# Branch A's product moved from the merge stage to the attention stage, and the order of the other two branches exchanged

## The chip, the cores and the metric

The kernel runs on one core of one Trainium2 chip. The metric is the device time of one execution in microseconds. Before the change it was 2761.7 us, the median of three runs (2759.91 to 2764.09).

The engines are called by their names in the profile: PE (TensorE, matmuls), PEld (the loading of its weights), DVE (VectorE), ACT (ScalarE), POOL (GpSimd) and SP (the engine that issues every DMA of this kernel, in one queue). Each engine works its own queue in order; semaphores tie the queues together.

## The reference

A block of two layers runs over 768 tokens: 256 of a context and 512 latent ones. Each layer projects its normalised input once, feeds three mixers, gates and sums their outputs, and goes on to an output projection and an MLP. What matters here:

```python
for l in range(DEPTH):                       # DEPTH = 2
    ...
    ya, yc = attend_queries(proj, ...)       # A: grouped-query attention, C: latent attention, 512 channels each
    ...
    ys = s5_glu(ys, u, s5_d[l], s5_w_glu[l]) # B: state-space scan, then gelu, product, a * sigmoid(g)
    mix = merge_branches(proj, ya, ys, yc, lp)
    x_mid = post_norm(x, g1 * mix, ...)
    ff = squared_relu_mlp(...)

def merge_branches(proj, ya, ys, yc, lp):
    g = sigmoid(proj[..., OFF_GATE:]).reshape(bsz, L, 3, 1024)
    merged = (g[..., 0, :] * (ya @ w_branch_a)
              + g[..., 1, :] * (ys @ w_branch_s5)
              + g[..., 2, :] * (yc @ w_branch_c))
    return merged @ w_out
```

Layer 0 computes all 768 tokens; layer 1 needs the output of the 512 latent ones only.

## The kernel before

**Products.** Channels lie on the partitions, tokens along the free dimension. Every large product is done in three passes of fp32r: weights and inputs are each split into a high part (a cast on ACT, line 151 for weights) and a low part (a subtraction, line 124 on DVE or line 154 on POOL), and `mm3` (lines 165 to 169) issues high x high, high x low and low x high into one PSUM group. `weights` (line 131) loads a block of weights into a `wr` tile and splits it into `wh` and `wl` tiles.

**Stages of a layer.** `layer` (line 362) runs the projections, then the attention stage (lines 1385 to 1404), then the merge stage (1407 to 1430), then `tail` with the output projection and the MLP. The layer's input lies in two tiles of [128, 8, 768], a high and a low half, in the pool `hp` with tag `h` and two buffers (lines 177 and 1247). The gates are the last to read them.

**Attention stage.** `attention` (line 913) runs through 8 heads of branch A, then 8 heads of branch C, block by block of 256 queries: scores on PE (line 872), maximum on DVE (875), exponential on ACT (878), scaling on DVE (880), transposes on PE (891), split on ACT and DVE (893, 894), product with V on PE (903, 904), sum of the halves (908, 909) and, for each second head, a DMA of the `yst` tile to the branch's DRAM tensor `brd[0]` or `brd[2]` (911). Beside it, `filler` (line 1398) issues the gates that the projection stage left over (`gates`, line 1122: blocks 9 to 23 in layer 0, 10 to 23 in layer 1; a block is 24 matmuls for each chunk of tokens, a tanh on ACT at line 1132 and a DMA to the DRAM tensor `gd`) and the S5 readout (`s5_readout`, line 1046: eight steps of copies on POOL, 24 small matmuls at lines 1070 and 1073, and an evacuation on ACT at line 1075 that goes to `Yd`). All gate blocks but one stand ahead of the readout in the program, the last behind it. Gates, S5 states and readout share the PSUM pool `gate`, which has one bank here (line 1394). Before the readout can start, a scan of 95 steps on POOL must have ended (lines 1036 to 1043).

**Merge stage.** `merge_branches` (line 1136) takes the branches in the order 0 (A), 1 (B), 2 (C). For A and C it loads the 512 channels from `brd` as four tiles `gt` and splits them (1152, 1153). For B it calls `s5_glu` (line 1079), which loads the readout from `Yd`, computes gelu with ACT and DVE (1088 to 1094), multiplies by the GLU's weights and forms the gated output (1096 to 1115). Then each branch runs 8 blocks of 128 output channels: 12 matmuls per chunk of tokens (chunks are two of 384 in layer 0 and one of 512 in layer 1, line 1119), a load of the gate tile `sg`, and an evacuation on DVE (line 1171) that multiplies by one plus the gate's tanh. Branch A's result begins the eight tiles `part`; B and C add theirs on POOL (1175); C, as the last, also splits the sum into `merged` (1177). In layer 0, the scalars of the next layer's S5 (`s5_scalars`, a long chain of small DVE operations) are issued after 12 steps of the merge, and a modulation (`mods`, line 278, lines 309 and 329) runs beside the rest.

**What sets the order.** The program's order gives each instruction a priority; `later` (line 107) lowers it. A planner works through a simulated timeline and puts, on each engine, the ready instruction of best priority next; the resulting queues are fixed. `mixed` (line 46) sets the program's order: it interleaves generators by the cost that they yield, divided by a weight. Buffers of a pool are taken in turn, and a tile that lies in memory of a closed pool waits for the tiles that lay there.

Of the kernel before, what the change touches and what calls it, by code (L numbers as in the profile page):

```python
# [13 lines left out]
F32 = mybir.dt.float32  # L14
F32R = mybir.dt.float32r
AF = mybir.ActivationFunctionType
ALU = mybir.AluOpType
# [4 lines left out]
P = 128  # L22
D = 1024
SEQ = 512
CTX = 256
T = SEQ + CTX
NT = T // P
EPS = 1e-6
DEPTH = 2
ALPHA = float((2.0 * DEPTH) ** 0.25)  # L30
GRID_W = 64
NCH = T // 8
# [13 lines left out]
def mixed(*gens):  # L46

    live = [[g, w, 0.0] for g, w in gens]
    while live:
        live.sort(key=lambda e: e[2])  # L50
        e = live[0]
        try:
            v = next(e[0])
        except StopIteration:
            live.remove(e)
            continue
        e[2] += v / e[1]
        yield v
# [7 lines left out]
def merge(*gens):  # L66
    drain(mixed(*gens))


class Block:  # L70
# [1005 lines left out]
            self.dma(out=self.Yd[:, 4 * q:4 * q + 4, 0:nn], in_=y)  # L1076
            yield 4.0

    def s5_glu(self, act, pool, l, out):

        nc = self.nc
        n0 = 0 if l < DEPTH - 1 else CTX // 8
        nn = NCH - n0
        glu = []
        for q in range(4):
            yt, t1, t2 = (self.tok(self.sgp, tag="gt").rearrange("p (i n) -> p i n", i=8) for _ in range(3))
            self.dma(out=yt, in_=self.Yd.rearrange("(i c) g n -> (c g) i n", c=16)[q * P:(q + 1) * P, :, 0:nn])
            nc.scalar.activation(t1, yt, AF.Square)
            nc.vector.tensor_scalar(out=t1, in0=t1, scalar1=0.044715, scalar2=1.0, op0=ALU.mult, op1=ALU.add)
            nc.vector.tensor_tensor(out=t1, in0=t1, in1=yt, op=ALU.mult)  # L1090
            nc.scalar.activation(t2, t1, AF.Tanh, scale=float(np.sqrt(2.0 / np.pi)))
            nc.vector.scalar_tensor_tensor(out=t1, in0=t2, scalar=1.0, in1=yt, op0=ALU.add, op1=ALU.mult)
            gH, gL = (self.tok(pool, F32R).rearrange("p (i n) -> p i n", i=8) for _ in range(2))
            self.half_split(gH, gL, t1)
            glu.append((gH, gL))
        wsrc = self.I["w_glu"][l].rearrange("(k p) (h c) -> p k h c", p=P, h=2)
        step = 4 if nn == NCH else 8
        for m in range(4):
            w = self.weights(([(h, wsrc[:, :, h, m * P:(m + 1) * P]) for h in range(2)], [P, 4, 2, P]), 256)
            ys = self.tok(self.sgp, tag="ys")  # L1100
            yv = ys.rearrange("p (n i) -> p i n", i=8)[:, ::-1, :]
            for i0 in range(0, 8, step):
                pss = []
                for h in range(2):
                    ps = self.bank([P, step, nn])
                    self.mm_k(ps, [([x[:, h, :] for x in w[k]], [x[:, i0:i0 + step, :] for x in glu[k]])
                                   for k in range(4)])
                    pss.append(ps)
                t1 = self.tok(self.sgp, tag="gt")[:, 0:step * nn].rearrange("p (i n) -> p i n", n=nn)
                nc.scalar.activation(t1, pss[1], AF.Tanh, scale=0.5)  # L1110
                nc.vector.scalar_tensor_tensor(out=yv[:, i0:i0 + step, :], in0=t1, scalar=1.0, in1=pss[0],
                                               op0=ALU.add, op1=ALU.mult)
            yh, yl = self.tok(act, F32R), self.tok(act, F32R)
            self.half_split(yh, yl, ys)
            out.append((yh, yl))
            yield 3.0
# [5 lines left out]
    def gates(self, l, hT, blocks, pools):  # L1122

        nc = self.nc
        for m in blocks:
            g0 = OFF_GATE + m * P
            wg = self.weights(self.I["w_in"][l, :, g0:g0 + P].rearrange("(k p) c -> p k c", p=P), P, pools)
            for t0, n in self.chunks(l):
# [4 lines left out]
                self.dma(out=self.gd[m, :, t0:t0 + n], in_=sg)  # L1133
                yield 24 * n / 2500.0

    def merge_branches(self, l, act, pool, merged):

        nc = self.nc
        c0 = self.chunks(l)[0][0]
        part = [None] * 8  # L1140
        for n, b in enumerate((0, 1, 2)):
            if b == 1:
                y = []
                yield from self.s5_glu(act, pool, l, y)
            else:
                y = []
                for k in range(4):
                    raw = self.tok(self.sgp, tag="gt")
                    self.dma(out=raw, in_=self.brd[b][k * P:(k + 1) * P, c0:])
                    yp = act if n == 0 else pool  # L1150
                    yh, yl = self.tok(yp, F32R), self.tok(yp, F32R)
                    nc.scalar.copy(yh, raw)  # L1152
                    self.split_low(yl, raw, yh)
                    y.append((yh, yl))
            wb = self.I[("wba", "wbs", "wbc")[b]][l].rearrange("(k p) c -> p k c", p=P)
            for m in range(8):
                if m % 2 == 0:
                    wbu = self.weights(wb[:, :, m * P:(m + 2) * P], 256)
                sg = self.tok(self.sgp, tag="sg")
                self.dma(out=sg, in_=self.gd[b * 8 + m, :, c0:])  # L1160
                if n == 0:
                    part[m] = self.tok(pool)
                if n == 2:
                    merged.append((self.tok(act, F32R), self.tok(act, F32R)))
                for t0, cnt in self.chunks(l):
                    ts = slice(t0 - c0, t0 - c0 + cnt)
                    pr = self.bank([P, cnt])
                    ms = slice((m % 2) * P, (m % 2) * P + P)
                    self.mm_k(pr, [([w[:, ms] for w in wbu[k]], [x[:, ts] for x in y[k]]) for k in range(4)])
                    o = part[m][:, ts] if n == 0 else sg[:, ts]  # L1170
                    nc.vector.scalar_tensor_tensor(out=o, in0=sg[:, ts], scalar=1.0, in1=pr, op0=ALU.add,
                                                   op1=ALU.mult)
                    if n == 0:
                        continue
                    nc.gpsimd.tensor_tensor(out=part[m][:, ts], in0=part[m][:, ts], in1=sg[:, ts], op=ALU.add)
                    if n == 2:
                        self.half_split(merged[m][0][:, ts], merged[m][1][:, ts], part[m][:, ts])
                yield 1.5


    def bcast_row(self, rows, src):
# [180 lines left out]
    def layer(self, l, hT, stop):  # L1362
        nc = self.nc
        last = l == DEPTH - 1
        nx = (9, 10)[l]
        with ExitStack() as c1:
# [18 lines left out]
            with ExitStack() as c2:  # L1385
# [10 lines left out]
                drain(self.s5_states(sp, l, slots))  # L1396

                def filler():
                    half = nx + (14, 13)[l]
                    yield from self.later(self.gates(l, hT, range(nx, half), wg), 200)  # L1400
                    yield from self.later(self.s5_readout(sp, l, slots), 0)
                    yield from self.later(self.gates(l, hT, range(half, 24), wg), 200)

                merge((self.attention(arena, l, per), 235.0 if not last else 180.0), (filler(), (170.0, 100.0)[l]))
        if stop == f"attn{l}":
            return
        self.c0 = c0 = self.chunks(l)[0][0]
        with ExitStack() as c1:
# [5 lines left out]
            with ExitStack() as c2:  # L1414
# [5 lines left out]
                if not last:  # L1420
                    for _ in range(12):
                        next(main)
                    self.s5_scalars(sp, _Carve(self, self.sgp, "gt"), l + 1)
                work = [(main, 42.0)]
                if not last:
                    self.mod_pools(c2, 2, 1)
                    self.lows = (1, 2)
# [113 lines left out]
```

## Time and profile before

| | |
|---|---|
| median of three runs | 2761.7 us |
| the profiled execution | 2761.72 us, its span 2759.9 us |
| mean granted clock of PE | 0.962 |
| first score product of the attention, layer 0 | 412.0 us |
| last write of the attention's output, layer 0 and layer 1 | issued at 790.66 and 2228.45 us |
| first product of the merge, layer 0 and layer 1 | 793.05 and 2227.65 us |
| first product with the output weights, layer 0 | 944.72 us |
| last evacuation of the merge (line 1171), layer 1 | 2327.34 us |

Times inside the execution count from the first instruction. A row of the stretches gives, for each engine, its busy time in the stretch and the number of its instructions; the granted clock is the share of full speed at which PE was let run. A row of the timeline gives start, duration, engine, line, operation, output and inputs, and in brackets how long the engine had been idle before it and what ended that. A row of the groups gives all instructions of one line and shape: busy time and mean duration in ns, then the idle time before them and what ended it. Matmuls are pipelined: their durations overlap, and the distance from start to start is what one costs.

### The profile page before, as it was taken

The page shows a single profiled execution, that of the slowest core. Times are in us where ns is not written, and L with a number is a line of the kernel's source. Part 1 is how long each engine was busy: PE and PEld are TensorE (multiplying, and loading weights), DVE is VectorE, ACT ScalarE, POOL GpSimd, SP SyncE. Part 2 cuts the span into 40 slices and gives each one's busy share as a digit, 9 for nine tenths or more (in the row PEclk, how much of TensorE's full clock was granted, in tenths as well). Part 3 has the DMA queues.
Part 4 walks back from the last instruction along what each step waited for, and adds up shares of the span by engine and source line. Part 5 has one row for each costly group of instructions (what it writes and reads, how often), then busy time and mean ns, then how long its engine had stood idle before and what let it go on. Part 6 is the DMA issues. An engine that isn't in the chain of part 4 may idle for free.

```text
span 2759.9 us, 45140 instructions
## 1 busy us (share of the span) xinstructions
PE 2570.2 (93%) x16128; PEld 2380.6 (86%) x16128; DVE 1794.7 (65%) x3338; ACT 1197.2 (43%) x2420; POOL 1167.4 (42%) x1698
## 2 busy tenths in 40 slices
PE   7999998999899989999999988998998989799997
PEld 4989898999899878999999988997877868688886
DVE  7998535777778678456668574455766757844345
ACT  4333367655543235132322234457654633533332
POOL 2378313870202577445446361310785004722224
PEclk9989998999999999999999999999999989899999
DMA  8665666333464535334535256457433445433332
GB/s 242 203 191 154 173 180 178 109 98 114 156 197 127 197 124 172 98 101 141 151 111 157 90 160 175 118 152 209 131 100 118 136 149 176 137 108 106 107 100 84
DMA packets 485312, 395.40 MB, mean 143 GB/s; under 512 B 103624, under 2 KB 413128, under 8 KB 485088
## 3 DMA queue, kind: packets, MB, share of 16 engines
q1 hardware_dynamic: 485088, 392.53, 47.2%
q8 instruction: 127, 2.08, 0.3%
q14 instruction: 97, 0.79, 0.1%
HBM read 326.87 MB, written 70.67 MB: 144 GB/s over the span
## 4 chain that ended last, share of the span: by engine, by line
PE 62%; DVE 10%; POOL 10%; DMA 8%; ACT 4%; issue 4%; SPq 1%; POOLq 0%; DVEq 0%; ACTq 0%
PE b L168 17%; PE b L169 17%; PE b L167 17%; PE sc L872 3%; DVE acc L309 2%; DVE wl L124 2%; PE b L891 2%; DMA wm<-w_mod 2%; POOL slots L1043 1%; POOL sc L1040 1%; POOL sc L1042 1%; POOL sc L1041 1%; DMA wr<-w_in 1%; PE b L904 1%; PE b L903 1%
## 5 line engine op out<-in xcount | busy, mean ns | idle before, releaser
L151 ACT CAST wh<-wr 128x512 fp32r<-128x512 f32 (+1 forms) x672 | 410.0, 619 | 739.8 <-PE b L168 278.5
L124 DVE TENSOR_TENSOR wl<-wr,wh 128x512 fp32r<-128x512 f32 (+2 forms) x612 | 486.7, 807 | 293.4 <-ACT wh L151 282.7
L167 PE MATMUL b<-h,wh 128*128 128x384 f32 (+2 forms) x1712 | 597.4, 350 | 18.8 <-ACT wh L151 11.0
L169 PE MATMUL b<-h,wl 128*128 128x384 f32 (+2 forms) x1712 | 593.1, 347 | 7.8 <-DVE wl L124 7.6
L168 PE MATMUL b<-h,wh 128*128 128x384 f32 (+2 forms) x1712 | 594.7, 348 | 5.5 <-POOL h L393 4.4
L168 PE MATMUL b<-wl,a 128*128 128x256 f32 (+1 forms) x1460 | 446.9, 310 | 10.5 <-DVE wl L124 9.1
L169 PE MATMUL b<-wh,a 128*128 128x256 f32 (+1 forms) x1460 | 444.9, 308 | 0.0
L167 PE MATMUL b<-wh,a 128*128 128x256 f32 (+1 forms) x1460 | 438.4, 309 | 6.1 <-ACT a L643 3.8
L167 PEld LDWEIGHTS b<-h,wh 128*128 128x128 f32 x1712 | 327.6, 192 | 38.0 <-ACT wh L151 12.3
L169 PEld LDWEIGHTS b<-h,wl 128*128 128x128 f32 x1712 | 326.9, 191 | 27.9 <-DVE wl L124 12.2
L168 PEld LDWEIGHTS b<-h,wh 128*128 128x128 f32 x1712 | 327.4, 191 | 24.3 <-POOL h L393 6.0
L168 PEld LDWEIGHTS b<-wl,a 128*128 128x128 f32 x1460 | 280.0, 192 | 25.9 <-DVE wl L124 11.6
L167 PEld LDWEIGHTS b<-wh,a 128*128 128x128 f32 x1460 | 276.0, 192 | 22.5 <-ACT a L643 3.9
L1201 POOL TENSOR_TENSOR acc<-acc,tmp 128x256 f32<-128x256 f32 (+1 forms) x160 | 170.4, 1068 | 285.9 <-DVE tmp L1200 272.7
L169 PEld LDWEIGHTS b<-wh,a 128*128 128x128 f32 x1460 | 280.0, 192 | 12.5
L309 DVE SCALAR_TENSOR_TENSOR acc<-wm,silu,acc 128x512 f32<-128x512 f32 x236 | 194.6, 845 | 29.3 <-DMA wm<-w_mod 26.5
L1226 POOL TENSOR_TENSOR sq<-r 128x384 f32<-128x384 f32 (+2 forms) x102 | 99.0, 972 | 239.3 <-ACT r L1224 226.5
L1200 DVE TENSOR_TENSOR tmp<-b,bc 128x256 f32<-128x256 f32 (+1 forms) x160 | 77.2, 484 | 168.8 <-PE b L169 151.3
L894 DVE TENSOR_TENSOR pt<-b,pt 128x512 fp32r<-128x512 f32 x208 | 141.9, 685 | 33.2 <-ACT pt L893 31.7
L875 DVE TENSOR_REDUCE mx<-sc 128x1 f32<-128x768 f32 (+1 forms) x160 | 134.1, 844 | 34.3 <-PE sc L872 33.4
L167 PE MATMUL b<-a,wh 128*128 128x384 f32 (+1 forms) x384 | 131.2, 369 | 16.6 <-ACT a L1152 11.8
L878 ACT ACTIVATE p<-sc,mx 128x768 f32<-128x768 f32 (+1 forms) x160 | 131.5, 823 | 34.4 <-PE b L891 19.4
(377 smaller groups left out, 5138.8 us busy)
## 6 DMA issues: line engine op xcount, KB each, us to landing
wr<-w_in SPq DMA_DIRECT2D x84, 512.0 KB, 4.2
wr<-w_up SPq DMA_DIRECT2D x76, 512.0 KB, 5.1
wr<-w_down SPq DMA_DIRECT2D x74, 512.0 KB, 3.8
wm<-w_mod SPq DMA_DIRECT2D x64, 512.0 KB, 4.7
wm<-w_mod SPq DMA_DIRECT2D x64, 256.0 KB, 2.9
wr<-w_out SPq DMA_DIRECT2D x26, 512.0 KB, 3.8
gd<-sg SPq DMA_DIRECT2D x48, 192.0 KB, 3.1
sg<-gd SPq DMA_DIRECT2D x24, 384.0 KB, 3.3
```

What stands on the lines that cost most here:

```text
L124: self.nc.vector.tensor_tensor(out=out, in0=src, in1=hi, op=ALU.subtract)
L151: self.nc.scalar.copy(h, raw[:, j0:j0 + jj])
L167: mm(ps, lhsT=a[0], rhs=b[0], start=start, stop=False)
L168: mm(ps, lhsT=a[0], rhs=b[1], start=False, stop=False)
L169: mm(ps, lhsT=a[1], rhs=b[0], start=False, stop=stop)
L309: i = nc.vector.scalar_tensor_tensor(out=acc, in0=w, scalar=s, in1=acc, op0=ALU.mult, op1=ALU.add)
L872: nc.tensor.matmul(sc[:, n0:n1], lhsT=q[:, qs], rhs=k[:, n0:n1], start=i == 0, stop=i == len(passes) - 1)
L875: nc.vector.reduce_max(out=mx, in_=sc[:, 0:nkey], axis=AX.X, negate=True)
L878: nc.scalar.activation(pt, sc[:, 0:nkey], AF.Exp, bias=mx, accum_out=sm)
L894: nc.vector.tensor_tensor(out=lo, in0=ps, in1=hi, op=ALU.subtract)
L1201: nc.gpsimd.tensor_tensor(out=r[t][:, cs], in0=r[t][:, cs], in1=tmp, op=ALU.add)
L1226: nc.gpsimd.tensor_tensor(out=sq, in0=rl, in1=rl, op=ALU.mult)
```

## The change

Branch A's product becomes a generator of its own, `branch_a`, which runs as the last part of the attention stage's filler. Its inputs (high and low) and its results `part` lie in two tiles with the layer's input's tag `h`; they can be written once the last gate has read that input. It loads the channels of `brd[0]` chunk by chunk through the tiles `sg`, splits them, and multiplies with weights through the attention stage's own small weight pool `wg`, into the one bank `gate`; gates are read back from `gd`. To make this possible all gates now stand ahead of the readout.

The merge stage begins with branch C; the GLU's gelu, split off as `s5_gelu`, is issued beside C's products. Then follow the GLU's product and branch B's product, which now splits the sum into `merged`. The results of the GLU lie in the pool of branch C's input instead of `act`. In layer 0 the next layer's S5 scalars are still issued after 12 steps, which now end before the GLU's product instead of after it. Three weights of `mixed` and `merge` change.

```diff
-    def s5_glu(self, act, pool, l, out):
+    def s5_gelu(self, pool, l, glu):
...
             glu.append((gH, gL))
+            yield 1.0
+
+    def s5_glu(self, pool, l, glu, out):
...
-            yh, yl = self.tok(act, F32R), self.tok(act, F32R)
+            yh, yl = self.tok(pool, F32R), self.tok(pool, F32R)
...
+    def branch_a(self, l, wg):
+
+        nc = self.nc
+        c0, n = self.chunks(l)[0]
+        size = T - c0
+        ys = self.t(self.hp, [P, 8, T], F32R, "h")
+        y = [(ys[:, k, 0:size], ys[:, 4 + k, 0:size]) for k in range(4)]
+        ps = self.t(self.hp, [P, 8, T], F32, "h")
+        self.part = [ps[:, m, 0:size] for m in range(8)]
+        for k in range(4):
+            for t0 in range(0, size, n):
+                raw = self.t(self.sgp, [P, n], F32, "sg")
+                ts = slice(t0, t0 + n)
+                self.dma(out=raw, in_=self.brd[0][k * P:(k + 1) * P, c0 + t0:c0 + t0 + n])
+                nc.scalar.copy(y[k][0][:, ts], raw)
+                self.split_low(y[k][1][:, ts], raw, y[k][0][:, ts])
+        yield 0.5
+        for m in range(8):
+            if m % 2 == 0:
+                wbu = self.weights(self.I["wba"][l].rearrange("(k p) c -> p k c", p=P)[:, :, m * P:(m + 2) * P], 256, wg)
+            ms = slice((m % 2) * P, (m % 2) * P + P)
+            for t0 in range(0, size, n):
+                ts = slice(t0, t0 + n)
+                sg = self.t(self.sgp, [P, n], F32, "sg")
+                self.dma(out=sg, in_=self.gd[m, :, c0 + t0:c0 + t0 + n])
+                pr = self.bank([P, n], which="gate")
+                self.mm_k(pr, [([w[:, ms] for w in wbu[k]], [x[:, ts] for x in y[k]]) for k in range(4)])
+                nc.vector.scalar_tensor_tensor(out=self.part[m][:, ts], in0=sg, scalar=1.0, in1=pr, op0=ALU.add,
+                                               op1=ALU.mult)
+            yield 12 * size / 2500.0
...
     def merge_branches(self, l, act, pool, merged):
...
+        y, glu = [], []
+        for k in range(4):
+            raw = self.tok(self.sgp, tag="gt")
+            self.dma(out=raw, in_=self.brd[2][k * P:(k + 1) * P, c0:])
+            yh, yl = self.tok(pool, F32R), self.tok(pool, F32R)
+            nc.scalar.copy(yh, raw)
+            self.split_low(yl, raw, yh)
+            y.append((yh, yl))
+        yield from mixed((self.products(l, 2, act, y, None), 12.0), (self.s5_gelu(pool, l, glu), 4.0 * 1.5))
+        y = []
+        yield from self.s5_glu(pool, l, glu, y)
+        yield from self.products(l, 1, act, y, merged)
...
                 def filler():
-                    half = nx + (14, 13)[l]
-                    yield from self.later(self.gates(l, hT, range(nx, half), wg), 200)
+                    yield from self.later(self.gates(l, hT, range(nx, 24), wg), 200)
                     yield from self.later(self.s5_readout(sp, l, slots), 0)
-                    yield from self.later(self.gates(l, hT, range(half, 24), wg), 200)
-
-                merge((self.attention(arena, l, per), 235.0 if not last else 180.0), (filler(), (170.0, 100.0)[l]))
+                    yield from self.later(self.branch_a(l, wg), 200)
+
+                merge((self.attention(arena, l, per), 235.0 if not last else 180.0), (filler(), (172.0, 122.0)[l]))
...
-                work = [(main, 42.0)]
+                work = [(main, 40.0)]
```

The new `products(l, b, act, y, merged)` holds the loop over the 8 blocks as it stood in `merge_branches`, for branches C and B: the weights, the gate's load, the 12 matmuls per chunk, the evacuation, the addition on POOL and, where `merged` is given, the split.

More of the change, by code (lines that the diff above doesn't have):

```diff
@@ L1077, in s5_readout @@
             yield 4.0
-    def s5_glu(self, act, pool, l, out):
+    def s5_gelu(self, pool, l, glu):
         nc = self.nc
-        n0 = 0 if l < DEPTH - 1 else CTX // 8
-        nn = NCH - n0
-        glu = []
+        nn = NCH if l < DEPTH - 1 else NCH - CTX // 8
         for q in range(4):
@@ L1095, in s5_glu @@
             glu.append((gH, gL))
+            yield 1.0
+    def s5_glu(self, pool, l, glu, out):
+        nc = self.nc
+        nn = NCH if l < DEPTH - 1 else NCH - CTX // 8
         wsrc = self.I["w_glu"][l].rearrange("(k p) (h c) -> p k h c", p=P, h=2)
@@ L1134, in gates @@
                 yield 24 * n / 2500.0
+    def branch_a(self, l, wg):
+        nc = self.nc
+        c0, n = self.chunks(l)[0]
[25 more added lines that the diff above has]
+            yield 12 * size / 2500.0
     def merge_branches(self, l, act, pool, merged):
@@ L1139, in merge_branches @@
         c0 = self.chunks(l)[0][0]
[L1140 to L1178, printed above, removed]
@@ new lines, in merge_branches, with products @@
+        yield from self.products(l, 1, act, y, merged)
+    def products(self, l, b, act, y, merged):
+        nc = self.nc
+        c0 = self.chunks(l)[0][0]
+        wb = self.I[("wba", "wbs", "wbc")[b]][l].rearrange("(k p) c -> p k c", p=P)
+        for m in range(8):
+            if m % 2 == 0:
+                wbu = self.weights(wb[:, :, m * P:(m + 2) * P], 256)
+            sg = self.tok(self.sgp, tag="sg")
+            self.dma(out=sg, in_=self.gd[b * 8 + m, :, c0:])
+            if merged is not None:
+                merged.append((self.tok(act, F32R), self.tok(act, F32R)))
+            for t0, cnt in self.chunks(l):
+                ts = slice(t0 - c0, t0 - c0 + cnt)
+                pr = self.bank([P, cnt])
+                ms = slice((m % 2) * P, (m % 2) * P + P)
+                self.mm_k(pr, [([w[:, ms] for w in wbu[k]], [x[:, ts] for x in y[k]]) for k in range(4)])
+                nc.vector.scalar_tensor_tensor(out=sg[:, ts], in0=sg[:, ts], scalar=1.0, in1=pr, op0=ALU.add,
+                                               op1=ALU.mult)
+                part = self.part[m][:, ts]
+                nc.gpsimd.tensor_tensor(out=part, in0=part, in1=sg[:, ts], op=ALU.add)
+                if merged is not None:
+                    self.half_split(merged[m][0][:, ts], merged[m][1][:, ts], part)
+            yield 1.5
```

## The prediction

> **What bounds the kernel now.** The page's first part comes first, for which engine is full:
>
> ```profile
> span 2759.9 us, 45140 instructions
> PE 2570.2 (93%) x16128; PEld 2380.6 (86%) x16128; DVE 1794.7 (65%) x3338; ACT 1197.2 (43%) x2420; POOL 1167.4 (42%) x1698
> ```
>
> PE is busy for 93%. The change leaves its work as it is, so only PE's idle and slowed time can be won. The busy time by stretches shows where that lies. Columns: stretch, its length, busy us and (instructions) of PE, PEld, DVE, ACT, POOL, the granted clock, DMA share, GB/s.
>
> ```profile
> 460.00:690.00 230.00, 228.65 (x1525) 222.85 (x1525) 165.88 (x344) 131.09 (x313) 133.23 (x374) 1.00 0.37 111
> 690.00:780.00 90.00, 80.95 (x616) 76.49 (x615) 69.96 (x140) 52.60 (x127) 24.38 (x23) 1.00 0.49 155
> 780.00:790.00 10.00, 8.94 (x61) 8.27 (x59) 4.12 (x7) 3.42 (x8) 0.00 (x0) 1.00 0.15 52
> 790.00:800.00 10.00, 6.95 (x27) 6.95 (x28) 3.84 (x5) 3.33 (x4) 0.00 (x0) 0.66 0.96 332
> 800.00:840.00 40.00, 39.99 (x228) 38.51 (x227) 36.35 (x58) 14.72 (x21) 0.99 (x2) 1.00 0.72 216
> 840.00:850.00 10.00, 6.20 (x27) 5.88 (x26) 8.72 (x13) 2.79 (x5) 0.00 (x0) 0.83 0.42 133
> ...
> 900.00:920.00 20.00, 16.00 (x74) 14.72 (x73) 13.88 (x25) 5.67 (x10) 16.92 (x19) 0.83 0.58 189
> ...
> 2077.00:2107.00 30.00, 18.57 (x122) 16.74 (x120) 18.36 (x35) 14.00 (x30) 23.36 (x64) 0.86 0.16 49
> 2107.00:2170.00 63.00, 60.97 (x456) 57.90 (x455) 45.12 (x91) 32.76 (x84) 16.34 (x14) 0.96 0.55 159
> 2170.00:2204.00 34.00, 32.80 (x212) 28.85 (x212) 26.96 (x52) 21.21 (x45) 0.00 (x0) 1.00 0.44 141
> 2204.00:2237.00 33.00, 19.02 (x82) 15.58 (x80) 15.51 (x27) 12.56 (x26) 0.00 (x0) 0.71 0.50 158
> ...
> 2240.00:2320.00 80.00, 78.99 (x344) 64.92 (x344) 57.53 (x82) 33.50 (x57) 18.98 (x13) 0.99 0.54 171
> ```
>
> Layer 0 first. With gates beside the attention (460 to 690) PE is full, so attention has no room there. With the readout beside it (690 to 790) PE idles 9.05 + 1.06 = 10.1 us. The merge stage (from 790) has three holes: 790 to 800, 840 to 850, 900 to 920. In layer 1 PE loses 11.4 us in 2077 to 2107, and in the attention's tail (2204 to 2237) 14.0 us, with the clock at 0.71. What PE waited for in these holes, over the whole run (us, times, longest):
>
> ```profile
> PE b L167 <- ACT a L1152: 11.8, 4, 5.6
> PE b L1073 <- POOL bsl L1063: 9.7, 1, 9.7
> PE b L167 <- ACT a L128: 4.8, 2, 3.8
> PE b L168 <- DVE a L124: 2.8, 2, 1.5
> ```
>
> L1152 and L124 on `a` are the merge's split of a branch's output, L128 the GLU's gelu, L1073 the S5 readout waiting for the scan on POOL. The timeline shows two of these turns closely:
>
> ```profile
> 778.86 0.34 PE L169 MATMUL b<-h,wl 128*128 128x384 f32 x1
> 780.39 0.34 PE L167 MATMUL b<-h,wh 128*128 128x384 f32 x1
> ...
> 788.87 0.28 PE L904 MATMUL b<-pt,v 128*128 128x256 f32 x1
> 793.05 2.61 PE L167 MATMUL b<-a,wh 128*128 128x384 f32 x7 [3.90 <-ACT a L1152]
> ...
> 790.66 0.38 SPq L78 DMA_DIRECT2D brd<-yst  x1
> ...
> 779.23 0.49 ACT L1132 ACTIVATE sg<-b 128x384 f32<-128x384 f32 x1 [1.79 <-PE b L169]
> 796.81 0.83 ACT L1152 CAST a<-gt 128x768 fp32r<-128x768 f32 x1 [0.41 <-DMA gt<-brd]
> ```
>
> The first pair and the ACT row at 779.23 are one turn of the single `gate` bank: a group ends at 779.20, is evacuated until 779.72, and the next begins at 780.39, 1.2 us after the end. The pair at 788.87 is the stage border: the attention's last product, then 3.9 us of nothing.
>
> **Order after the readout.** The last gate block stands behind the readout in the program, and runs behind it:
>
> ```profile
> 773.77 0.48 ACT L1075 COPY y<-b 128x384 f32<-128x384 f32 x1 [0.79 <-PE b L1073]
> ...
> L1075 ACT COPY y<-b x16: 372/429/487, 694.2 to 2170.5; 128x384 f32<-128x384 f32 x8, 128x256 f32<-128x256 f32 x8
> L1132 ACT ACTIVATE sg<-b x72: 480/495/629, 75.1 to 2181.3; 128x384 f32<-128x384 f32 x48, 128x512 f32<-128x512 f32 x24
> ```
>
> The readout's last evacuation is at 773.8 and 2170.5, the last gate's first evacuation at 779.2 in layer 0, its only one at 2181.3 in layer 1. With one bank, what stands behind the readout did not slip into it, though PE had idle time. Branch A's product now stands there. I take this order for it: after the readout, so in layer 0 nearly at the attention's end (788.9), in layer 1 some 55 us ahead of it.
>
> **What is moved.** Layer 0: 192 matmuls of 384 columns at 39.99 us / 228 = 0.175, 33.7 us. Layer 1: 96 of 512 at 78.99 / 344 = 0.230, 22.0 us. These leave the merge and come back in the attention stage. With them come, from these rows,
>
> ```profile
> L1171 DVE SCALAR_TENSOR_TENSOR sg<-sg,b 128x384 f32<-128x384 f32 x32 | 17.1, 547 | 5.8 <-DMA sg<-gd 5.8
> L124 DVE TENSOR_TENSOR wl<-wr,wh 128x512 fp32r<-128x512 f32 x29 | 22.4, 780 | 5.1 <-ACT wh L151 4.9
> L124 DVE TENSOR_TENSOR a<-gt,a 128x768 fp32r<-128x768 f32 x8 | 8.5, 1078 | 4.8 <-ACT a L1152 4.8
> L1171 DVE SCALAR_TENSOR_TENSOR a<-sg,b 128x512 f32<-128x512 f32 x8 | 5.5, 686 | 1.5 <-PE b L169 1.5
> ```
>
> on DVE in layer 0 16 x 0.547 + 8 x 0.780 + 8 x 0.54 (half of 1.078) = 19.3 us, in layer 1 8 x 0.686 + 8 x 0.780 + 4 x 0.69 = 14.5 us. DVE has 20.0 us free in 690 to 780 and 17.9 + 7.0 in 2107 to 2204, so it bears them, just. On SP layer 0 issues 12 more transfers (8 + 16 against 4 + 8) at the 0.38 us of the row at 790.66, 4.6 us, layer 1 none; queued behind them are the attention's loads of q. I cost this at nothing: the tiles are loaded two ahead, under the readout. If that cover fails, 4.6 us come on top.
>
> **Layer 0, the sum.** The 33.7 us come back in full, since the 10.1 us of idle lie mostly ahead of the branch's turn. To them comes the bank's turn: 16 groups x 1.2 us = 19.2 us if nothing fills it, 0 if the attention's tail or the third branch's product does; unknown, I take half, +9.6. What goes: at the border, branch groups run where PE had nothing, -3.9 and the slow clock's 6.95 - 27 x 0.175 = 2.2; and the split of the third branch, which came late behind the S5 scalars, is no longer in mid-stage: 4.0 idle (900 to 920) and 16.00 - 74 x 0.175 = 3.0. The gelu's wait (3.8 and 1.5) I keep: DVE was busy 45.07 of 50 us before it, and the third branch's product puts the same work beside it; it could go, or grow by the S5 scalars, which now stand ahead of the GLU's evacuations instead of behind. Sum -33.7 + 33.7 + 9.6 - 6.1 - 7.0 = -3.5; ends -13.1 - 10.1 = -23 (all filled) and +19.
>
> **Layer 1, the sum.** Two things change. The last gate block, 24 x 0.230 = 5.5 us, now stands ahead of the readout, in the 9.7 us that PE waits for POOL: -5.5 (ends 0 and -5.5; POOL's scan itself stays). Then 8 groups run from about 2170 on, beside the attention. There PE has 1.2 us, 14.0 less the border's
>
> ```profile
> 2237.45 0.79 PE L167 MATMUL b<-a,wh 128*128 128x512 f32 x1 [5.61 <-ACT a L1152]
> ```
>
> 5.6 us, and 19.02 x 0.29 = 5.5 of slow clock: 15.1. I take half, -7.5, as the attention's own chain (DVE, ACT, PE in turn) is delayed by each group that stands in its way. The new wait: the third branch's input now begins the merge, and its last quarter is the last head's output. How long transfers of these tiles take from issue to landing:
>
> ```profile
> DMA to landing us min/median/max: 1.7/1.8/5.7
> ```
>
> In layer 0 that write is issued at 790.66; two landings and the issue between them, about 5 us, bring the cast to 796, where the fourth cast stood anyway (796.81). Behind that load SP holds gate and gelu loads. In layer 1 the border already took from 2228 to 2237. So 0, at most +3 each. Sum -22.0 + 22.0 - 5.5 - 7.5 = -13.0; ends -20.6 and +3.
>
> **Together** -16.5 us against the profiled execution's 2761.72 (span 2759.9 and 1.8 around it), which equals the median 2761.7: **2745 us**.
>
> **The rivals.**
> B, both layers fill: the branch uses the bank between the readout's turns. Against it speaks the last gate, which did not; for it the 10.1 us. Then -16 in layer 0 and -18 in layer 1: 2728.
> C, moved and no more: attention is a chain through DVE, ACT and PE, and each group lengthens it by its own time; bank turns eat what the border gives. Layer 0 +6, layer 1 -6: 2762. For it: PE 97% busy in 2107 to 2204.
> D, slower: the branch isn't beside the attention at all but between it and the merge. The third branch's split inputs lie, by the order and sizes of the pools, largely in the bytes that the branch's own weights hold until its last matmul; if so, that product can't fill the turns. Price: 16 x 1.2 + 8 x 1.2 = 28.8, less the 7.0 and 5.5 that go in any case: +16, 2778. It decides where the branch's groups begin after the attention's last transposes; by 773.8 and 788.9 that is near in layer 0, not in layer 1.
>
> [...]
>
> **Chances.** Forecast 0.47 (its own range 2735 to 2756), B 0.16, C 0.18, D 0.19. Measurements of this kernel tell 0.2%, 5.5 us, from no change. Faster: B and nearly all of the forecast, 0.61; within 0.2%: C and the forecast's edge, 0.20; slower: D, 0.19. The range takes in B's 2728 and most of D: 2726 to 2775.
>
> **What would show it.** Right: the first branch's groups, told from the gates by their DVE evacuation into tiles named `h`, start right after the readout in both layers; no wait of 9.7 us on POOL but one near 4; no L124 wait in mid-merge in layer 0; layer 1's tail with PE over 80% busy at full clock; some of the 16 gaps of 1.2 us visible in layer 0. Wrong: branch matmuls between the readout's groups (B); these groups alone on PE after the last L904, each followed by a wait for DVE (D); a longer attention in layer 1 by more than 15 us (C); or a shift in stages that the change doesn't touch, as the planner orders the whole program anew.

## The result: slower by 0.7%, all of it in layer 0

The changed kernel takes 2783.2 us (median of four runs, 2781.45 to 2783.57) against 2762.0 us for the kernel before: ratio 1.0074, 95% interval 1.0062 to 1.0086. The prediction said 2745 us, with a range that ended at 2775.

The first part of the page of the changed kernel:

```profile
span 2781.2 us, 45157 instructions
PE 2572.3 (92%) x16128; PEld 2378.4 (86%) x16128; DVE 1798.2 (65%) x3342; ACT 1198.6 (43%) x2424; POOL 1180.3 (42%) x1698
```

PE is busy for 2.1 us more than before and the span is 21.3 us longer: the time was lost as idle time of PE. Three lines mark where. L872 is a score product, L909 the last step before the attention's output is written, L382 the first transposes of the norm behind the output projection. The rows are from the view of a line, once per layer; the pair of times is the start of the first and of the last.

```profile
L872 PE MATMUL sc<-k,q x320: 276/286/775, 412.3 to 784.2; 128*128 128x512 f32 x128, 128*128 128x256 f32 x32
L909 DVE TENSOR_TENSOR yst<-b,ytmp x48: 397/422/429, 434.7 to 800.4; 64x256 f32<-64x256 f32 x48
L382 PE MATMUL b<-ident,xh x48: 270/273/477, 1027.5 to 1077.2; 128*128 128x128 f32 x48
L872 PE MATMUL sc<-k,q x256: 274/390/788, 1920.5 to 2251.8; 128*128 128x512 f32 x128
L909 DVE TENSOR_TENSOR yst<-b,ytmp x32: 404/422/429, 1945.9 to 2271.2; 64x256 f32<-64x256 f32 x32
L382 PE MATMUL b<-ident,xh x32: 270/418/477, 2394.7 to 2423.0; 128*128 128x128 f32 x32
```

From first L872 to last L909 is a layer's attention stage (800.4 - 412.3 = 388.1), from there to the last L382 its merge stage with the output projection (1077.2 - 800.4 = 276.8). The same six marks in every kernel of this study give the table; "between" is from layer 0's last L382 to layer 1's first score, stages that the change does not touch. The start (410 to 415 us) and what follows the last L382 (358.0 to 358.6 us) are alike in all and left out. The stages are those of the one profiled execution; the time is the median of all executions, and the ratio is to the kernel before, measured beside it on the same chip (2762 to 2765 us). Executions of one kernel lie up to 20 us apart (e4, 2759.5 to 2779.5), and the profiled ones of e3, e6, e12 and e13 5 to 8 us from their medians, so a stage difference of a few us in one trace is not shown.

| kernel | att. 0 | merge 0 | between | att. 1 | merge 1 | us | ratio (95%) |
|---|---|---|---|---|---|---|---|
| before | 377.6 | 265.3 | 844.1 | 328.0 | 174.9 | 2762.0 | |
| after | 388.1 | 276.8 | 843.3 | 350.7 | 151.8 | 2783.2 | 1.0074 (1.0062, 1.0086) |
| e10_order_only | 376.4 | 262.2 | 846.8 | 326.6 | 174.3 | 2761.3 | 0.9995 (0.9982, 1.0008) |
| e5_layer1_only | 379.1 | 262.7 | 838.8 | 354.3 | 152.3 | 2758.1 | 0.9977 (0.9966, 0.9988) |
| e8_l1_ba_first | 378.8 | 262.4 | 839.2 | 330.3 | 151.5 | 2734.4 | 0.9889 (0.9874, 0.9904) |
| e11_split_gates0 | 378.6 | 265.1 | 844.3 | 323.1 | 155.1 | 2736.2 | 0.9909 (0.9892, 0.9925) |
| e6_ba_first | 390.8 | 277.3 | 843.8 | 328.2 | 153.2 | 2761.7 | 0.9998 (0.9985, 1.0010) |
| e12_ahead_both | 378.6 | 313.0 | 846.7 | 322.4 | 153.7 | 2782.2 | 1.0075 (1.0057, 1.0094) |
| e7_mods_behind | 387.8 | 271.5 | 845.1 | 352.9 | 152.2 | 2781.0 | 1.0051 (1.0036, 1.0066) |
| e1_banks | 386.4 | 273.1 | 844.9 | 342.4 | 177.3 | 2792.3 | 1.0091 (1.0076, 1.0106) |
| e2_sgu | 387.6 | 272.4 | 850.3 | 342.2 | 154.3 | 2778.6 | 1.0047 (1.0030, 1.0064) |
| e3_sgu_act | 385.9 | 262.3 | 844.5 | 349.2 | 156.1 | 2777.6 | 1.0045 (1.0031, 1.0060) |
| e4_sgu_act_banks0 | 385.4 | 262.0 | 839.9 | 354.4 | 157.7 | 2769.8 | 1.0022 (1.0007, 1.0037) |
| e13_both_mended | 388.3 | 262.1 | 840.4 | 329.3 | 158.6 | 2748.5 | 0.9947 (0.9929, 0.9965) |

In the changed kernel layer 0 loses 10.5 us in its attention and 11.5 in its merge. Layer 1 gives 23.1 us less of merge for 22.7 us more of attention: nothing.

**Layer 0 after.** The stretches between attention and merge, with the columns known from before:

```profile
800.00:820.00 20.00, 13.29 (x57) 11.86 (x58) 12.13 (x20) 1.58 (x3) 0.00 (x0) 0.83 0.66 221
820.00:840.00 20.00, 13.33 (x56) 10.40 (x55) 12.05 (x20) 2.42 (x4) 1.05 (x2) 0.91 0.45 138
840.00:860.00 20.00, 13.23 (x47) 10.62 (x48) 9.02 (x14) 2.84 (x4) 0.00 (x0) 0.77 0.39 133
860.00:880.00 20.00, 20.00 (x114) 20.00 (x113) 16.79 (x22) 9.44 (x13) 8.07 (x6) 0.97 0.50 144
```

For 60 us PE runs at two thirds, with a slowed clock, where before had 800 to 840 full. What PE waited for between 785 and 900 (us, times, longest):

```profile
PE b L167 <- DVE h L1167: 15.1, 10, 3.5
PE b L167 <- ACT a L1180: 4.4, 1, 4.4
```

L1167 on tiles `h` is the evacuation of branch A's product, L1180 the cast of branch C's input. Two turns in the timeline, first PE, then DVE:

```profile
805.20 0.34 PE L169 MATMUL b<-h,wl 128*128 128x384 f32 x1
806.19 0.44 PE L167 MATMUL b<-h,wh 128*128 128x384 f32 x1 [0.65 <-DVE h L1167]
...
808.22 0.34 PE L169 MATMUL b<-h,wl 128*128 128x384 f32 x1
812.01 0.44 PE L167 MATMUL b<-h,wh 128*128 128x384 f32 x1 [3.46 <-DVE h L1167]
```
```profile
805.58 0.56 DVE L1167 SCALAR_TENSOR_TENSOR h<-sg,b 128x384 f32<-128x384 f32 x1 [1.05 <-PE b L169]
808.75 2.74 DVE L309 SCALAR_TENSOR_TENSOR acc<-wm,silu,acc 128x512 f32<-128x512 f32 x4 [2.62 <-DMA wm<-w_mod]
811.41 0.55 DVE L1167 SCALAR_TENSOR_TENSOR h<-sg,b 128x384 f32<-128x384 f32 x1
```

The group that ends at 805.5 is evacuated at once, and the next starts 0.65 us after its end. The one that ends at 808.6 finds four additions of the modulation (L309) in front on DVE, which had themselves waited 2.62 us for a load, and the next group starts 3.5 us after its end. That is rival D's picture, with a price that D did not have: the queue in front of the evacuation.

### The profile page after: what moved, and what is told of

Same layout as the page of the kernel before. It is cut to its first block, busy times and chain, and to the rows that moved or that the text cites. A ratio compares the mean times of both kernels' runs of the same rounds, so it can differ in the third digit from the quotient of the medians.

```text
span 2781.2 us, 45157 instructions
## 1 busy us (share of the span) xinstructions
PE 2572.3 (92%) x16128; PEld 2378.4 (86%) x16128; DVE 1798.2 (65%) x3342; ACT 1198.6 (43%) x2424; POOL 1180.3 (42%) x1698
## 4 chain that ended last, share of the span: by engine, by line
PE 62%; DVE 12%; POOL 9%; DMA 6%; issue 5%; ACT 4%; SPq 2%; POOLq 0%; DVEq 0%; ACTq 0%
PE b L167 17%; PE b L168 17%; PE b L169 17%; PE sc L872 3%; DVE wl L124 2%; PE b L891 2%; DMA wm<-w_mod 2%; DVE acc L309 2%; SPq L78 2%; PE b L904 1%; PE b L903 1%; PE b L1073 1%; POOL sc L1040 1%; POOL sc L1042 1%; POOL slots L1043 1%
## 5 line engine op out<-in xcount | busy, mean ns | idle before, releaser
L151 ACT CAST wh<-wr 128x512 fp32r<-128x512 f32 (+1 forms) x672 | 410.0, 619 | 707.9 <-PE b L169 269.6
L167 PE MATMUL b<-h,wh 128*128 128x384 f32 (+2 forms) x1808 | 633.6, 351 | 31.7 <-DVE h L1167 15.1
L169 PE MATMUL b<-h,wl 128*128 128x384 f32 (+2 forms) x1808 | 627.8, 348 | 7.3 <-DVE wl L124 7.2
L168 PE MATMUL b<-h,wh 128*128 128x384 f32 (+2 forms) x1808 | 629.5, 349 | 5.3 <-POOL h L393 4.4
L167 PE MATMUL b<-wh,a 128*128 128x256 f32 (+1 forms) x1460 | 440.5, 311 | 11.5 <-ACT wh L151 4.7
L167 PEld LDWEIGHTS b<-h,wh 128*128 128x128 f32 x1808 | 345.8, 192 | 57.4 <-DVE h L1167 16.1
L169 PEld LDWEIGHTS b<-h,wl 128*128 128x128 f32 x1808 | 345.3, 191 | 28.2 <-DVE wl L124 11.2
L168 PEld LDWEIGHTS b<-h,wh 128*128 128x128 f32 x1808 | 345.8, 191 | 24.9 <-POOL h L393 5.9
L167 PEld LDWEIGHTS b<-wh,a 128*128 128x128 f32 x1460 | 277.3, 193 | 27.1 <-ACT wh L151 5.2
L309 DVE SCALAR_TENSOR_TENSOR acc<-wm,silu,acc 128x512 f32<-128x512 f32 x236 | 193.5, 841 | 34.7 <-DMA wm<-w_mod 31.2
L872 PE MATMUL sc<-k,q 128*128 128x512 f32 (+1 forms) x576 | 140.1, 357 | 9.0 <-ACT p L878 6.5
L1208 POOL TENSOR_TENSOR h<-h,sg 128x384 f32<-128x384 f32 (+1 forms) x48 | 64.3, 1361 | 192.7 <-DVE sg L1205 189.9
```

The lines of the kernel that those rows point to most:

```text
L151: self.nc.scalar.copy(h, raw[:, j0:j0 + jj])
L167: mm(ps, lhsT=a[0], rhs=b[0], start=start, stop=False)
L168: mm(ps, lhsT=a[0], rhs=b[1], start=False, stop=False)
L169: mm(ps, lhsT=a[1], rhs=b[0], start=False, stop=stop)
L309: i = nc.vector.scalar_tensor_tensor(out=acc, in0=w, scalar=s, in1=acc, op0=ALU.mult, op1=ALU.add)
L872: nc.tensor.matmul(sc[:, n0:n1], lhsT=q[:, qs], rhs=k[:, n0:n1], start=i == 0, stop=i == len(passes) - 1)
```

## The experiments

Each run is read in the stage it was made for, since a total also holds shifts elsewhere.

**Which layer loses: layer 0 undone (e5_layer1_only).** Branch A's product goes back into the merge in layer 0, in front of C's; layer 1 stays as changed. The S5 scalars stand ahead of the GLU, as in the change, not behind it, as the expectation has it: their step L486 comes at 876.6, just before the GLU's first evacuation at 877.6, while before it came at 897.6, after the GLU's last at 870.3.

```diff
-                    yield from self.later(self.branch_a(l, wg), 200)
+                    if last:
+                        yield from self.later(self.branch_a(l, wg), 200)
...
+        if l == 0:
...
+            yield from self.products(l, 0, act, y, None)
```

> Layer 0 keeps branch A's product in the merge stage, ahead of branch C's; its S5 scalars stand behind the GLU as before the change; layer 1 is as changed. Theory: the whole loss of 21 us arises in layer 0 from branch A's groups running alone behind the attention, and layer 1 nets nothing (its branch groups delay the attention's end by the 22 us that the merge saves); then 2758 to 2768. Rival: the exchanged order of branches C and B, which stays here, costs most of it; then 2773 or more. Rival 2: layer 1 is worth a gain that layer 0 hides; then below 2755.

Measured 2758.1 us, at the lower end of the theory's range. Layer 0 takes 641.8 us against 642.9 before and 664.9 after: the whole loss is there. Layer 1 takes 506.6 against 502.9: moved and no more, or a little worse.

**What the turns are made of (e1_banks, e7_mods_behind, e2_sgu).** e1 gives branch A the three banks of the pool `pv`, which the attention's transposes and products with V use:

```diff
-                pr = self.bank([P, n], which="gate")
+                pr = self.bank([P, n], which="pv")
```

> The changed kernel with one edit: branch A's groups take the attention's three pv banks instead of the one gate bank. Theory (turns of one bank): layer 0's 16 groups, 65 us in the changed kernel, pass in 34 to 42 us, 20 to 25 us less, and the time is 2756 to 2766. Rival (the groups are slow for another reason, their gate loads through two tiles or DVE's queue): the groups keep 55 us or more and the time stays within 6 us of 2783.

e7 puts layer 0's modulation on DVE behind the branch's last evacuation:

```diff
-                nc.vector.scalar_tensor_tensor(out=self.part[m][:, ts], in0=sg, scalar=1.0, in1=pr, op0=ALU.add,
+                self.ba_last = nc.vector.scalar_tensor_tensor(out=self.part[m][:, ts], in0=sg, scalar=1.0, in1=pr, op0=ALU.add,
...
-                    work.append((self.later(self.mods(l, (5,), kk=1, eager=True), 100), 16.0 * 1.1))
+                    work.append((self.later(self.mods(l, (5,), kk=1, eager=True), 100, (self.ba_last.ins,)), 16.0 * 1.1))
```

> The changed kernel with one edit: on DVE the layer 0 modulation (32 products of 0.75 us) is queued behind branch A's last evacuation. Theory: evacuations that stood behind pairs of these (1.4 us) come earlier, a turn falls from 4.1 us towards 3.3, 16 turns give 8 to 12 us; as the work must be done later beside the GLU, half of it stays: 2773 to 2779. Rival: the turns are set by PE and the bank alone; then 2781 to 2787, or more where the modulation is late.

e2 takes branch A's gate loads out of the `sg` tiles, which the first load of the merge waited for:

```diff
-                sg = self.t(self.sgp, [P, n], F32, "sg")
+                sg = self.t(sp, [P, n], F32, "u")
```

> The changed kernel with one edit: branch A's gate loads go through the readout's u tiles instead of the sg tiles, in whose memory the first tiles of the merge (gt, the third branch's loads) lie. Theory: the third branch could not start because gt waited for the last sg; now it is loaded at the attention's end (about 803 instead of 854 us) and its product fills the turns of the bank: 2758 to 2768. Rival: its split inputs lie in the memory of branch A's weights as well, so the loads come early but the product not; then within 5 us of 2783. In layer 1 no change by either.

The waits of PE between 790 and 840 us, in e1 and then in e7:

```profile
PE b L167 <- ACT a L1180: 4.2, 1, 4.2
PE b L167 <- DVE h L1167: 1.8, 3, 1.1
```
```profile
PE b L167 <- DVE h L1167: 7.9, 12, 0.9
PE b L167 <- ACT a L1180: 4.7, 1, 4.7
```

With three banks the turn is gone (15.1 to 1.8 us). With one bank and DVE free it is about 0.65 us (7.9 us in twelve waits, the longest 0.92), and the branch is done at 835 instead of 854 us. So of the 15.1 us about half was the bank and half the queue on DVE. Yet layer 0's merge gets only 3.7 us shorter in e1 and 5.3 in e7. In e1 the 16 evacuations pass in 36 us instead of 65, as its theory said, but the gain is lost again behind them: from 840.6 to 867.5 us DVE works without a pause, and PE waits for the GLU's tanh (L1114) and for an evacuation in the merge (L1205). Its waits in e1 between 850 and 960 us:

```profile
PE b L167 <- ACT gt L1114: 6.1, 1, 6.1
PE b L167 <- DVE sg L1205: 4.4, 2, 4.0
```

In e7 the modulation that no longer stands in front stands beside the gelu and the GLU later (PE then waits 7.2 us for L1114), and its total, 2781.0, lies at the edge of the rival's. The turn was real, but DVE's work behind it looks like a second limit. In layer 1, to which e1's edit also applies, branch A falls behind the attention, which shares these banks: its last evacuation starts at 2283.9, after the last yst of 2257.0, and merge 1 is 177.3 us, as long as before the change. That is why e1 is the slowest of all, far from its theory's 2766. In e2 the load was issued early (784 us), but C's cast still came at 852.5, and PE went on waiting 15.2 us for L1167; its 2778.6 us are the rival's.

**Whether C's product can fill the turns (e3_sgu_act, e4_sgu_act_banks0).** In e2 the split inputs of C still lay over the weights that branch A was using. e3 moves them to `act`; e4 adds the three banks, in layer 0 alone.

```diff
-            yh, yl = self.tok(pool, F32R), self.tok(pool, F32R)
+            yh, yl = self.tok(act, F32R), self.tok(act, F32R)
```
```diff
-                pr = self.bank([P, n], which="gate")
+                pr = self.bank([P, n], which="pv" if l == 0 else "gate")
```

> Both layers as changed, but the first branch's gate loads land in the readout's u tiles, and the third branch's split inputs (L1180) are written to the tiles of act, which overlie no weights of the first branch, in place of a3's first eight, which do. Theory (the third product was kept off the bank turns only because its inputs lie over weights still in use): its groups lie between the first branch's, PE is busy for over 8.5 of each 10 us between 800 and 850, and what the turns cost (65 us for 16 turns with 34 us of matmuls in them) is got back but for a few us: LN transposes after layer 0 (L382) by 1005 to 1010, total 2758 to 2768 beside a before of 2762. Rival (the turn itself is the price: DVE's modulation and ACT's casts stand in front of the evacuations and of the splits alike): the splits come no earlier than 840, L382 stays at 1020 to 1025, total 2775 to 2782.

> As e3_sgu_act, and in layer 0 alone the first branch's groups take the three banks of the attention's readout instead of the one gate bank. Theory (two independent losses in layer 0: inputs over weights, and one bank): L382 at or below 1005, 4 to 10 us earlier than with the inputs moved alone, total 2752 to 2764. Rival (either edit alone fills the same gap): L382 within 3 us of e3_sgu_act or of e1_banks (1019.2), total no lower than the lower of these two.

The casts of C's input in e3, then PE's timeline there:

```profile
L1180 ACT CAST a<-gt x4: 829/832/835, 797.5 to 806.7; 128x768 fp32r<-128x768 f32 x4
```
```profile
840.39 0.69 PE L167 MATMUL b<-h,wh 128*128 128x384 f32 x1 [2.19 <-DVE h L1167]
...
844.07 0.34 PE L167 MATMUL b<-a,wh 128*128 128x384 f32 x1
```

The inputs are there over 50 us earlier than in the changed kernel (857.0 to 861.6), the load of C's first weights is issued at 773.1, and still the first product of C stands on PE right behind branch A's last, with no wait before it; between the groups PE waits 13.1 us for L1167. So the memory was not what kept C out of the turns: PE's queue is fixed, and the planner had put C behind A. What e3 wins in its trace (merge 0 at 262.3 instead of 276.8, 14.5 us) is in part that C starts without the wait of 4.4 us; branch A's last evacuation also comes 6.3 us sooner after the attention (46.8 instead of 53.1), and the rest lies behind. e4 takes the turns away as well (2.6 us of L1167 left) and its merge 0 is no shorter, 262.0. So e3's theory falls: PE is busy for 6.0 to 8.8 of each 10 us between 800 and 840, where it asked for over 8.5, and the total of 2777.6 us is the rival's, though the rival's late splits (840 us) did not come either. e4's theory falls too, its layer 0 being 647.4 us against 648.2, and its rival, a total no lower than e3's or e1's, is not met either. Their medians are 7.8 us apart, but the profiled execution of e3 is its shortest of seven (2769.6 us) and no longer than e4's, so these traces can't show where that difference lies, and e3's stage times hold for that execution alone.

**The order alone (e10_order_only).** Filler, gate order and weights as before; A's product in the merge, in front of C with the gelu beside it, then the GLU, then B.

> Before's filler, gate order and weights of the merge; in both layers the first branch's product stays in the merge, ahead of the third's with the gelu beside it, then the GLU, then the second's (the order of the change without the move beside the attention; the S5 scalars after 20 steps). Theory (the move is the whole loss, the new order of the merge costs nothing in itself): layer 0 ends (L382) at 1004 to 1008, total 2755 to 2764. Rival (the new order loses, because before's GLU stood between two products and its chain lay beside them): L382 at 1012 or later as in e5_layer1_only (1013.1), and the merge of layer 1 some us longer, total 2768 to 2775.

Measured 2761.3, no change; layer 0 is 4.3 us shorter than before, layer 1 by 2.0, and 2.7 us come back between. The new order costs nothing, and the move is what is left.

**Another place in layer 1 (e8_l1_ba_first, e6_ba_first).** One exchange of two lines: branch A's product is handed out in front of the readout. e8 does it on e5, e6 on the change itself.

```diff
+                    if last:
+                        yield from self.later(self.branch_a(l, wg), 200)
                     yield from self.later(self.s5_readout(sp, l, slots), 0)
-                    if last:
-                        yield from self.later(self.branch_a(l, wg), 200)
```

> As e5_layer1_only (layer 0's first product back in the merge, ahead of the third; layer 1 as changed), with one difference: in layer 1 the first branch's product is handed out ahead of the scan's readout instead of behind it. Theory (layer 1 gains nothing because PE still waits 14.8 us for POOL's bsl at the first readout, at a place where the branch could run but is handed out later): that wait goes to under 3 us, the first score of layer 1 to the end falls from 864.6 to about 850, total about 2745 beside 2758.1. Rival (what PE does not wait for there it waits for later: the readout then ends behind the attention and the gelu waits for Yd; or the attention's own chain is the limit): first score to end 858 or more, total 2752 to 2762.

> The change as it is, with one difference: in layer 1 alone the first branch's product is handed out ahead of the scan's readout. Theory (the place in layer 1 is worth the same whatever layer 0 does; e8_l1_ba_first took first score to last yst write from 354.3 to 330.3): that stretch falls from 350.7 to about 330, layer 0 stays (last L382 near 1077), total about 2763. Rival (e8_l1_ba_first's gain came from layer 0's return to before, through the order of later stages): total 2775 or more.

Both theories held, e8's by more than it said: attention 1 falls by 24.0 us against e5, and in e6 by 22.5 against the change. e8 is the fastest kernel here, 1.1% below before. The stretch around the first step of the readout, which comes 204 to 214 us after the first score, in before, after and e8:

```profile
2088.00:2128.00 40.00, 29.71 (x197) 27.80 (x196) 22.91 (x39) 16.84 (x38) 18.55 (x42) 0.83 0.34 99
```
```profile
2110.00:2150.00 40.00, 25.14 (x155) 23.47 (x154) 20.46 (x37) 15.84 (x35) 24.98 (x60) 0.74 0.41 125
```
```profile
2082.00:2122.00 40.00, 38.09 (x225) 33.19 (x224) 35.72 (x63) 24.52 (x51) 21.71 (x55) 0.96 0.54 154
```

PE's idle time there is 10.3 us before, 14.9 after, 1.9 in e8, and the clock 0.83, 0.74 and 0.96. The row of waits behind it in the changed kernel, and branch A's evacuations in layer 1, in the changed kernel and then in e8, where PE doesn't wait for bsl at all:

```profile
PE b L1073 <- POOL bsl L1063: 14.6, 1, 14.6
```
```profile
L1167 DVE SCALAR_TENSOR_TENSOR h<-sg,b x8: 681/688/689, 2208.7 to 2251.5; 128x512 f32<-128x512 f32 x8
```
```profile
L1167 DVE SCALAR_TENSOR_TENSOR h<-sg,b x8: 678/688/689, 2102.7 to 2141.1; 128x512 f32<-128x512 f32 x8
```

In e8 the branch runs where PE had waited for POOL, its first evacuation 210 us after the first score; in the changed kernel it comes at 288 us, 78 us later.

**The same place in layer 0 (e12_ahead_both).** The exchange of e8 in both layers, on the change.

> The change as it is, with one difference: in both layers the first branch's product is handed out ahead of the scan's readout instead of behind it. Theory (what layer 0 loses is that the branch's one-bank groups run alone after the attention; handed out earlier they run beside it, and what is left for the end is the readout): the waits of L167 for L1167 in layer 0 under 2 us in all, the last LN transpose of layer 0 at 1055 to 1065 instead of 1077.2, and with layer 1's gain of about 20 us a total of 2738 to 2748. Rival (layer 0's attention leaves PE no free time, and the readout at its end has turns of its own and holds up the gelu, so that the loss changes its place only): last L382 at 1070 or later, total 2752 to 2765.

Layer 1 wins as in e8 (322.4), and layer 0's attention is as short as before (378.6). But the readout is now what is left over: its evacuations run from 804.3 to 881.8, after the attention, and merge 0 is 313.0. A row of PE's waits between 790 and 900, and two stretches of the same kernel:

```profile
PE b L1070 <- DMA m<-Md: 33.1, 7, 10.5
```
```profile
500.00:600.00 100.00, 98.72 (x659) 96.21 (x657) 72.67 (x157) 58.09 (x144) 85.95 (x240) 1.00 0.36 105
600.00:700.00 100.00, 99.69 (x661) 96.77 (x662) 72.55 (x154) 56.61 (x142) 14.99 (x39) 1.00 0.37 109
```

Layer 0's attention has next to no free PE time there, so whichever part is handed out last runs alone behind it. The readout is worse there than the branch, since seven of its eight steps wait for a load. The rival is right and its price was too low: layer 0 takes 691.6 us, 26.7 more than in the change.

**What a mended move is worth (e13_both_mended), and layer 0's gates (e11_split_gates0).** e13 is e4 with branch A in front of the readout in layer 1. e11 is e8 with layer 0's last block of gates behind the readout, as before. (Its expectation speaks of four; the edit moves one block, whose two groups are evacuated at 779.7 and 787.2 us, behind the readout's last at 774.2.)

> As e4_sgu_act_banks0 (layer 0: three banks for the branch, the third's inputs in act, gate loads in u), and in layer 1 the branch's product ahead of the readout. Theory (both places add up): 2769.8 less 20, about 2750, still above e8_l1_ba_first's 2734.4 because layer 0's attention has no free PE time to sell: PE busy there is 98 to 100 us of each 100 between 500 and 700. Rival (with layer 0 mended the move pays there too, and e4 lost only in layer 1): 2738 or less.

> As e8_l1_ba_first, with layer 0's gates again as before: four of the ten behind the scan's readout instead of all ahead of it, and its filler's weight 170 again. Theory (in layer 0 the exchange of gates and readout costs a few us by itself: there the readout's last evacuation came 14 us later, 787.9 against 774.0 in e10_order_only): layer 0's last LN transpose (L382) at 1050 to 1053 and a total of 2728 to 2734 beside 2734.4. Rival (layer 0's merge takes the late readout without loss, since the gelu now lies beside the third product): total 2733 to 2738.

e13 comes out at 2748.5, as its theory had it: with layer 0's move mended in three ways the kernel still takes 14 us more than e8, which leaves layer 0's product in the merge. In the two traces, 19.5 us apart, 9.2 us are layer 0 (650.4 against 641.2) and 6.1 layer 1 (487.9 against 481.8), where e13 also has C's inputs and the gate loads elsewhere. e11 takes 2736.2 us, within the rival's range: where this block of gates stands makes no difference that these runs can tell.

## Why the prediction was wrong

**The moved work: right.** The 22.0 us left layer 1's merge (23.1 measured) and came back in its attention. In layer 0 four of 16 groups were evacuated before the attention's end (788.6 to 799.6 us), and the attention took 10.5 us longer, 4 x 2.1 = 8.4 of it for their work: the full price.

**The place: right.** The first evacuation comes at 788.6, behind the readout's last at 785.1, and at 2208.7 behind 2204.9.

**Layer 0's bank turn, +9.6: the step that failed.** I took 1.2 us for each of 16 turns and let half of them be filled. From the attention's end (800.4) to the branch's (854.1, when its last evacuation ends and C's load is issued) the other 12 groups take 53.7 us, of which 12 x 2.1 = 25.2 are work: 28.5 us over, where I had 9.6 for all 16. Of these 15.1 are the waits, about 7 the slowed clock (0.84 over these 53.7 us; by the starts of these matmuls, of which 34 are 0.32 us apart instead of 0.17), and 3 the modulation's own matmuls (L329), which before had in the merge too. A bare turn was cheaper than I had it, 0.65 us of wait (e7); what I left out is that the evacuating engine serves the modulation at the same time, and that with waits of 2 to 3.5 us the clock was slower. And nothing filled the turns. Rival D named the right place, but its reason, C's inputs over A's weights, was not enough: in e3 they lay elsewhere, and the order on PE was the same. My range ended at 2775, below D's own 2778, though it was said to take in most of D. Taking the turns away alone gave back 5.4 us of layer 0's 22.0 (e1) or 5.6 (e7); with C's inputs and the gate loads elsewhere as well it was 17.5 (e4). What share belongs to the turns and what to DVE's work behind them stays open.

**Layer 0's -6.1 at the border and -7.0 in mid-merge: won in part.** From 854.1 to its last L382 the changed kernel takes 223.1 us. Before took 265.3 from the attention's end, 231.6 without branch A's 33.7: 8.5 us more, 3 of them the matmuls of L329. So some 5 of the 13.1 us came, and the sum closes: 2.1 more in the attention, 28.5 behind it and 8.5 less in the rest make 22.1, measured 22.0. PE is full from 790 to the attention's end at 800.4 (10.2 of 10.4 us), as said; but the border's load and cast now stand behind the branch (4.4 us for L1180), and PE waits for the GLU (2.5 us for L1114) and a cast of weights (4.2 for L151) instead. By e10 the order alone is worth 4.3 us in layer 0.

**Layer 1's -5.5 and -7.5: the second step that failed, both nothing.** Of -13.0 us -0.4 came (502.5 against 502.9), and rival C's sign, an attention longer by over 15 us, is there. The gate block did move ahead, but the wait for POOL grew from 9.7 to 14.6 us. The scan's last step came 212.0 us after the first score instead of 202.6, but in e2 it came at 203.8 and the wait was 15.7 us; no run separates the gates' place from the filler's weight (122 instead of 100), and why the wait grew is open. The attention's tail took each branch group in full: PE was busy from 2200 to 2250 without a gap, and the last score came 331.3 us after the first instead of 304.7. The stretch in the changed kernel:

```profile
2200.00:2250.00 50.00, 50.00 (x310) 44.60 (x308) 39.73 (x69) 26.37 (x55) 0.00 (x0) 1.00 0.42 129
```

So my sign of a full tail at full clock came, and yet no time was won: the tail was filled and grew by what filled it. I had seen both holes; the change put the work in neither. e8 shows that the 9.7 us hole was worth having and sat in front of the readout, not behind it.

**The gaps and the clock.** The forecast and rival D both price a turn at its 1.2 us, with nothing for the clock. That fits e7, whose waits of about 0.65 us went with a clock of 1.00 from 800 to 830 us, but not the changed kernel, where it was 0.77 to 0.91 from 800 to 860, as the last section shows.

**The stages between** moved by -0.8 us here; other variants show 838.8 to 850.3 there, in one execution each. Whether this is the planner's order or the spread between executions is open; differences of 5 us in a total say little without the stages.

## What to carry to other kernels

Before moving work beside a chain, find the stretch where the full engine idles and check that the program hands the moved work out there, not merely in the same stage: the same 22 us lengthened the attention by 22.7 behind the readout and by at most 2.3 in front of it (e8; 0.2 in e6). Where PE was busy for 98.7 and 99.7 us of 100, as in layer 0 (e12), the work handed out last ran alone at the end, with one bank and whatever else the evacuating engine had in its queue. Read a long program by marks between stages, since totals mix the move with shifts elsewhere.

## What the runs showed of the hardware

In the stretches below, the granted clock was 1.00 in e7, where no wait between groups was over 0.92 us, and 0.91 and 0.92 in e3, where the longest wait was 2.0 us in the first and 2.2 us (838.2 to 840.4) at the end of the second:

```profile
800.00:810.00 10.00, 7.79 (x42) 6.83 (x41) 2.36 (x4) 1.24 (x2) 0.00 (x0) 1.00 0.77 266
810.00:820.00 10.00, 7.61 (x40) 6.36 (x38) 3.24 (x6) 0.62 (x1) 0.00 (x0) 1.00 0.38 113
```
```profile
800.00:820.00 20.00, 12.91 (x61) 11.16 (x61) 17.13 (x28) 5.02 (x7) 0.00 (x0) 0.91 0.85 275
820.00:840.00 20.00, 14.85 (x64) 11.85 (x64) 14.56 (x23) 4.95 (x7) 0.99 (x2) 0.92 0.50 146
```

PE is busy for 76 to 78% in e7 with the clock at 1.00, and for 65 and 74% in e3 with 0.91 and 0.92; in the changed kernel, with waits up to 3.5 us between groups and one of 4.4 us for L1180, it is 0.83, 0.91 and 0.77 from 800 to 860. In the kernel before, three waits of 1.2 to 1.5 us within 6 us (900 to 920) went with 0.83. Whether the length of a wait decides or how many come close together, these runs don't separate.
